# A new order of the attention steps in a hybrid encoder layer: head 2's scores behind the last key tile and the latent keys' product, head 3's scores and the transposes one product later

## The chip, the cores and the metric

The kernel runs on one core of one Trainium2 chip. The metric is the device time of one execution in microseconds (us). The names of the engines are those of the profile: PE is TensorE (PEld its weight loads), DVE is VectorE, ACT is ScalarE, POOL is GpSimd, SP issues the loads.

## The reference

Two encoder layers on one sequence of 256 tokens and 2048 features, float32. Each layer has two groups of heads that share one input projection and one output projection, and an MLP behind them. Every sub-layer is scaled and shifted by a modulation computed from the vector `c`.

```python
for l in range(DEPTH):
    mod = cond @ w_ada[l] + b_ada[l]
    sh_a, sc_a, g_a, sh_m, sc_m, g_m = [m[:, None, :] for m in jnp.split(mod, 6, axis=-1)]
    h = _rmsnorm(x) * (1.0 + sc_a) + sh_a
    proj = h @ w_in[l]                      # dq, dk, dv, cq, ckv, kr are its columns
    ...
    out_a = _diff_attention(dq, dk, dv, positions, rel_bias_table, lam, diff_subln_g[l], lambda_init)
    q = (_rmsnorm(cq, q_norm_g[l]) @ w_uq[l]).reshape(B, S, MLA_HEADS, MLA_NOPE + MLA_ROPE)
    q_nope = q[..., :MLA_NOPE]
    q_rope = _rope(q[..., MLA_NOPE:], cos[:, :, None, :], sin[:, :, None, :])
    kv = (_rmsnorm(ckv, kv_norm_g[l]) @ w_ukv[l]).reshape(B, S, MLA_HEADS, MLA_NOPE + MLA_V)
    k_nope, v_m = kv[..., :MLA_NOPE], kv[..., MLA_NOPE:]
    k_rope = _rope(kr, cos, sin)
    out_b = _mla_attention(q_nope, q_rope, k_nope, k_rope, v_m)
    x = x + g_a * (jnp.concatenate([out_a, out_b], axis=-1) @ w_o[l])
    h = _rmsnorm(x) * (1.0 + sc_m) + sh_m
    x = x + g_m * (jnp.square(jax.nn.relu(h @ w_mlp_in[l])) @ w_mlp_out[l])
return _rmsnorm(x, final_norm_g)
```

The first group is differential attention: 4 heads, each with two softmaxes over the 256 keys with a bias, of which the second, times `lam`, is taken from the first; the values are 256 wide. The second group is latent attention (MLA): 8 heads whose queries come from a normalised 512-wide latent (`w_uq`), and whose keys and values come from a normalised 256-wide latent (`w_ukv`); a part of 64 columns is rotated by position.

## The kernel before

**Layout.** Features lie on the 128 partitions and the 256 tokens along the free dimension. A float32 weight tile is loaded as 128 x 2048 (`raw`, L152, five buffers) and split in two halves of 1024 columns into a high part (`hi`, ScalarE, L140) and a remainder (`lo`, VectorE, L141), four buffers of each. A product of weights and activations is three matmuls: `hi` with the activation's high and low part and `lo` with the high part (L176 to L178, or L251 to L253 where the tokens are the output's partitions).

**adaLN sums.** The modulation is not made on TensorE. Each 128 x 2048 tile of `w_ada` is loaded (L287) into the same five `raw` buffers and multiplied and summed on VectorE (L303). Each call of `weights` first emits the sums of the tiles that are there, and by a rate (`RATE_A0`, `RATE_A2`) now and then one more load, so these sums stand among all of VectorE's other work.

**The steps of the attention.** In the function `layer` (L646):

- `col(i)` makes one 128-wide tile of the queries or keys of the differential heads; every second one ends with a copy `k` on ScalarE (L270). Tiles 0 to 5 make the keys of heads 1, 2 and 3.
- `probs(hd)`, that is `diff_probs`, makes the scores of a head (tile `psc`, L897), adds the bias and takes the row minimum on VectorE (L898), exponentials on ScalarE (L884), then on VectorE the reciprocal (L887), the factor (L904), scaling and difference (L907, L908). Its result is `a[hd]`.
- `up_k`, `up_q(0)`, `up_q(1)`, `up_r` and `up_v` are products of the latents with a loaded weight tile each: the MLA keys `kn`, the queries `qn` of heads 0 to 3 and 4 to 7, the part to be rotated `qr` (turned on TensorE with a permutation, tile `pqr`, L870, and finished on VectorE, L873 to L875), and the values `vm` (tile `pv`). The first four fill banks `pss`.
- `turn(hd)` transposes `a[hd]` on TensorE (tile `pt`, L915) and copies it to `aT` on ScalarE.
- `mla` is a list in which the three steps of the 8 MLA heads follow one another in a staggered order: `mla[0]` is head 0's scores (tile `psm`, L963 and L964, then VectorE L965, exponentials L884, and the scaling by the reciprocal on ScalarE, L968), `mla[1]` and `mla[2]` are head 1's scores and head 0's transpose, `mla[3:6]` are head 2's scores, head 1's transpose and head 0's values (tile `pom`, L980).
- `val(cg, kq)` makes the values of the differential heads from the projected input; what is left of `mla` is spread among them.

**What sets the order.** The steps are written out by hand in the order of calls. The framework's planner takes that order as a priority, simulates the engines with its own costs, and puts an instruction that is ready at its planned time ahead of one that is not; what it plans is then each engine's fixed queue. The accumulators share eight banks (`pp`), the small tiles pools of 40 (`u`) and 6 (`t`).

Of the kernel before, what the change touches and what calls it, by code (L numbers as in the profile page):

```python
# [99 lines left out]
class Trunk:  # L100
# [545 lines left out]
    def layer(self, l, acc):  # L646
# [35 lines left out]
        def col(i, out, scale):  # L682
            def f():
                if i % 2 == 0:
                    self.ps = self.bank("ps")
                self.tile_cols(self.ps[:, i % 2], io["w_t"][l, i], h)
                if i % 2:
                    out.append(self.copy(self.ps, "k", scale))
            return f

        def up_k():
            kn.extend(self.copy(ps, "kn") for ps in self.small(io["w_uk"][l], ckv, 8))

        def up_q(b):
            qn.extend(self.copy(ps, "qn", ms) for ps in self.small(io["w_uq"][l, b], cq, 4))

        def up_r():
            raw = [self.copy(ps, "qr", ms) for ps in self.small(io["w_uq"][l, 2], cq, 4)]
            qr.extend(self.rope_q(x) for x in raw)

        def up_v():
            w = self.weights(io["w_uv"][l])
            for cg in range(2):
                pss = [self.bank("pv") for _ in range(2)]
                self.tokens_by_k(pss, [[z[:, 512 * cg : 512 * cg + 512] for z in y] for y in w], ckv, True, True)
                vm.append([self.copy(ps, "vm") for ps in pss])
# [12 lines left out]
        def probs(hd):  # L719
            return lambda: a.append(self.diff_probs(l, hd, q[hd], kk[hd]))  # L720

        def turn(hd):
            return lambda: at.append(self.transposed(a[hd]))
# [15 lines left out]
        for n, (i, dst, scale) in enumerate(order):  # L739
            col(i, dst, scale)()  # L740
            if n == 0:
                cq += self.latent(cqr, self.vec[:, V_QG + 4 * l : V_QG + 4 * l + 4])
            probs(n)()
            col(i + 1, dst, scale)()
        if l:
            self.rate = RATE_A2
        up_k()
        probs(3)()
        up_q(0)
        turn(0)()  # L750
        up_r()
        turn(1)()
        mla[0]()
        up_v()
        turn(2)()
        for f in mla[1:3]:
            f()
        up_q(1)
        turn(3)()
        for f in mla[3:6]:  # L760
            f()
# [312 lines left out]
```

## Time and profile before

| | |
|---|---|
| median of 3 runs | 2240.9 us (2237.83 to 2252.52) |
| profiled execution, its own time | 2238.34 us |
| its span, first to last instruction | 2236.6 us |
| busy PE / PEld | 98% / 88% |
| busy DVE / ACT / POOL | 74% / 50% / 0% |
| chain that ended last, PE's share | 92% |
| mean granted TensorE clock | 0.997 |
| DMA | 585.53 MB, mean 262 GB/s |

A row of a timeline has the start in us, the duration, the engine, the line, the operation, the tile written and those read, the shapes and a count; in brackets stands how long the engine was idle before it, and which instruction ended that. Matmuls overlap, so a matmul's duration is longer than the distance to the next one. A row of a grouped view has the count, then busy us and the mean ns of one, then the engine's idle time before such instructions.

### The profile page before, as it was taken

To read this page: it belongs to the slowest core of one execution; us is meant where nothing else is said; L and a number is where in the kernel's file an instruction comes from. 1 tells how busy PE (TensorE), PEld (TensorE's weight loads), DVE (VectorE), ACT (ScalarE), POOL (GpSimd) and SP (SyncE) were. 2 spreads that over 40 slices of the span, in tenths; PEclk is the share of its full clock that TensorE was granted. 3 is DMA by queue.
4 is the path that set the end of the run, shared out by engine and by line. 5 is a ranking of instruction groups with operands and counts; after the bars stand their busy time and mean duration, and the time that the engine had idled before them with its cause. 6 is when DMAs were issued, how large, how long until landed. Compare 5 with 4: busy or idle time off the path is not lost.

```text
span 2236.6 us, 33121 instructions
## 1 busy us (share of the span) xinstructions
PE 2195.2 (98%) x13362; PEld 1957.4 (88%) x13362; DVE 1665.8 (74%) x2275; ACT 1117.7 (50%) x1657; POOL 1.9 (0%) x10
## 2 busy tenths in 40 slices
PE   6899999999999999999999999999999999999998
PEld 5799889998888888888899988989888888888887
DVE  7879879988878888887888776775665565565565
ACT  4445664455454355355445465544635534544553
POOL 0000000000000000000000000000000000000000
PEclk9999999999999999999999999999999999999999
DMA  9898778898888888888779666655555555555551
GB/s 387 308 380 305 271 275 315 315 349 317 322 319 308 313 313 317 310 305 315 297 265 350 248 245 224 238 210 191 200 189 188 189 188 189 188 188 188 189 188 76
DMA packets 85692, 585.53 MB, mean 262 GB/s; under 512 B 9505, under 2 KB 9889, under 8 KB 21409
## 3 DMA queue, kind: packets, MB, share of 16 engines
q1 hardware_dynamic: 85538, 583.42, 70.1%
q8 instruction: 104, 1.70, 0.3%
q14 instruction: 50, 0.41, 0.0%
HBM read 581.28 MB, written 2.10 MB: 261 GB/s over the span
## 4 chain that ended last, share of the span: by engine, by line
PE 92%; DVE 4%; ACT 1%; issue 1%; DVEq 0%; ACTq 0%
PE ps L196 42%; PE ps L197 21%; PE pk L177 4%; PE pk L176 4%; PE pk L178 4%; PE pk L240 3%; DVE ada L303 2%; PE pv L252 1%; PE pv L251 1%; PE pv L253 1%; DVE lo L141 1%; PE ps L176 1%; PE ps L177 1%; PE ps L178 1%; PE pw L533 1%
## 5 line engine op out<-in xcount | busy, mean ns | idle before, releaser
L141 DVE TENSOR_TENSOR lo<-raw,hi 128x1024 fp32r<-128x1024 f32 (+1 forms) x722 | 853.8, 1185 | 430.1 <-ACT hi L140 426.1
L140 ACT ACTIVATE hi<-raw 128x1024 fp32r<-128x1024 f32 (+1 forms) x722 | 740.2, 1028 | 824.2 <-PE ps L196 610.7
L196 PE MATMUL ps<-hid,hi 128*128 128x512 f32 x2048 | 718.0, 395 | 0.0
L196 PE MATMUL ps<-h,hi 128*128 128x512 f32 x1664 | 581.5, 394 | 0.0
L197 PE MATMUL ps<-hid,lo 128*128 128x256 f32 x2048 | 573.4, 280 | 0.0
L197 PE MATMUL ps<-h,lo 128*128 128x256 f32 x1664 | 465.7, 280 | 0.0
L196 PEld LDWEIGHTS ps<-hid,hi 128*128 128x128 f32 x2048 | 384.0, 188 | 91.6 <-DVE hid L170 1.3
L303 DVE SCALAR_TENSOR_TENSOR ada<-ada,cond 128x2048 f32<-128x2048 f32 x192 | 437.8, 2283 | 2.8 <-DMA ada<-in_w_ada 2.7
L197 PEld LDWEIGHTS ps<-hid,lo 128*128 128x128 f32 x2048 | 386.7, 189 | 0.1
L196 PEld LDWEIGHTS ps<-h,hi 128*128 128x128 f32 x1664 | 311.9, 187 | 72.6
L197 PEld LDWEIGHTS ps<-h,lo 128*128 128x128 f32 x1664 | 314.1, 189 | 0.0
L177 PE MATMUL pk<-h,hi 128*128 128x256 f32 x704 | 199.0, 283 | 0.0
L178 PE MATMUL pk<-h,lo 128*128 128x256 f32 x704 | 198.9, 283 | 0.0
L176 PE MATMUL pk<-h,hi 128*128 128x256 f32 x704 | 198.5, 284 | 0.0
L834 DVE SCALAR_TENSOR_TENSOR x<-ps,mod,x 128x256 f32<-128x256 f32 x272 | 131.2, 483 | 65.2 <-PE ps L197 60.5
L177 PEld LDWEIGHTS pk<-h,hi 128*128 128x128 f32 x704 | 135.1, 192 | 0.1
L178 PEld LDWEIGHTS pk<-h,lo 128*128 128x128 f32 x704 | 135.1, 192 | 0.0
L176 PEld LDWEIGHTS pk<-h,hi 128*128 128x128 f32 x704 | 134.6, 192 | 0.1
L240 PE MATMUL pk<-hf,w 128*128 128x256 f32 x384 | 90.0, 398 | 11.5 <-ACT hf L547 11.5
L240 PEld LDWEIGHTS pk<-hf,w 128*128 128x128 f32 x384 | 76.6, 201 | 24.0 <-ACT hf L547 12.7
L196 PE MATMUL ps<-mo,hi 128*128 128x512 f32 x192 | 69.0, 399 | 0.0
L196 PE MATMUL ps<-do,hi 128*128 128x512 f32 x192 | 68.9, 399 | 0.0
(205 smaller groups left out, 2283.8 us busy)
## 6 DMA issues: line engine op xcount, KB each, us to landing
raw<-in_w_m SPq DMA_DIRECT2D x232, 1024.0 KB, 4.9
ada<-in_w_ada SPq DMA_DIRECT2D x192, 1024.0 KB, 4.9
raw<-in_w_ob SPq DMA_DIRECT2D x24, 1024.0 KB, 5.1
raw<-in_w_m SPq DMA_DIRECT2D x32, 768.0 KB, 4.4
raw<-in_w_dv SPq DMA_DIRECT2D x16, 1024.0 KB, 4.8
raw<-in_w_a SPq DMA_DIRECT2D x20, 768.0 KB, 6.3
raw<-in_w_t SPq DMA_DIRECT2D x12, 1024.0 KB, 4.8
w<-in_w_a SPq DMA_DIRECT2D x24, 384.0 KB, 8.9
```

The lines of the kernel that those rows point to most:

```text
L140: nc.scalar.activation(hi, v, AF.Copy)
L141: ins = nc.vector.tensor_tensor(lo, v, hi.bitcast(F32), ALU.subtract)
L176: mm(ps, hi, x[0], start=first, stop=False, skip_group_check=shared)
L177: mm(ps, hi, x[1], start=False, stop=False, skip_group_check=shared)
L178: mm(ps, lo, x[0], start=False, stop=last, skip_group_check=shared)
L196: mm(ps.rearrange("p a b -> p (a b)"), hi, both, start=k == 0, stop=False)
L197: mm(ps[:, 0], lo, x, start=False, stop=k == nk - 1)
L240: self.nc.tensor.matmul(ps, v, whole[k], start=first, stop=last, skip_group_check=True)
L251: mm(ps, xh, hi, start=first and k == 0, stop=False)
L252: mm(ps, xh, lo, start=False, stop=False)
L303: ins = nc.vector.scalar_tensor_tensor(w, w, 1.0, self.cond, ALU.mult, ALU.mult, accum_out=acc[:, i : i + 1])
L834: self.nc.vector.scalar_tensor_tensor(x, ps[i][:, j], g[:, m + i : m + i + 1], x, ALU.mult, ALU.add)
```

## The change

The order of the calls in `layer`, for both layers. `probs(2)` leaves the loop, where it stood between `col(4)` and `col(5)`, and follows `up_k()`. `probs(3)` follows `up_q(0)` instead of preceding it. `up_v()` precedes `mla[0]` instead of following it, and `up_q(1)` precedes `mla[1:3]`. No call is added or left out.

```diff
             col(i, dst, scale)()
             if n == 0:
                 cq += self.latent(cqr, self.vec[:, V_QG + 4 * l : V_QG + 4 * l + 4])
-            probs(n)()
+            if n < 2:
+                probs(n)()
             col(i + 1, dst, scale)()
         if l:
             self.rate = RATE_A2
         up_k()
+        probs(2)()
+        up_q(0)
         probs(3)()
-        up_q(0)
         turn(0)()
         up_r()
         turn(1)()
+        up_v()
         mla[0]()
-        up_v()
         turn(2)()
+        up_q(1)
         for f in mla[1:3]:
             f()
-        up_q(1)
         turn(3)()
         for f in mla[3:6]:
             f()
```

## The prediction

> **What bounds the kernel now.** I read the page first: the engines' busy shares and the chain of work that ended last.
>
> ```profile
> span 2236.6 us, 33121 instructions
> PE 2195.2 (98%) x13362; PEld 1957.4 (88%) x13362; DVE 1665.8 (74%) x2275; ACT 1117.7 (50%) x1657; POOL 1.9 (0%) x10
> ...
> PE 92%; DVE 4%; ACT 1%; issue 1%; DVEq 0%; ACTq 0%
> ```
>
> TensorE sets the time: 92% of the chain is PE. A new order of the same instructions can therefore only win what PE loses by waiting, in the stretch that the edit touches: the attention of layer 0 (about 200 to 262 us) and of layer 1 (about 1288 to 1345 us). Next come sums over stretches. Columns: length, then busy time with the count for PE, PEld, DVE, ACT, POOL, then granted clock, DMA share, GB/s.
>
> ```profile
> 172.00:216.00 44.00, 44.00 (x353) 43.40 (x352) 43.54 (x82) 25.44 (x45) 0.00 (x0) 1.00 0.81 304
> 216.00:224.00 8.00, 6.16 (x43) 5.54 (x43) 5.87 (x15) 5.48 (x15) 0.00 (x0) 1.00 0.73 277
> 224.00:248.00 24.00, 22.96 (x146) 19.46 (x145) 23.03 (x40) 15.23 (x29) 0.00 (x0) 1.00 0.71 268
> 1270.00:1326.00 56.00, 55.60 (x393) 51.20 (x393) 45.40 (x93) 33.66 (x67) 0.00 (x0) 1.00 0.66 245
> ```
>
> In layer 0 PE has two weak places, 216 to 224 and 224 to 248 us, and VectorE is full on both sides of the first (43.54 of 44, 23.03 of 24). In layer 1 PE is idle for 0.40 us of 56 and VectorE has room. PE's timeline names the holes of layer 0:
>
> ```profile
> 218.63 0.28 PE L178 MATMUL pss<-lath,lo 128*128 128x256 f32 x1
> 220.45 1.13 PE L897 MATMUL psc<-k,q 128*128 128x256 f32 x4 [1.54 <-ACT k L270]
> ...
> 221.53 0.28 PE L177 MATMUL pss<-latl,hi 128*128 128x256 f32 x1
> 221.65 0.28 PE L178 MATMUL pss<-lath,lo 128*128 128x256 f32 x1
> 222.23 0.70 PE L897 MATMUL psc<-k,q 128*128 128x256 f32 x2 [0.30 <-DVE mx L898]
> ...
> 234.81 2.13 PE L870 MATMUL pqr<-qr,K 128*128 128x512 f32 x4
> ...
> 238.81 0.40 PE L253 MATMUL pv<-hi,latl 128*128 128x512 f32 x1
> 239.04 0.39 PE L251 MATMUL pv<-hi,lath 128*128 128x512 f32 x1
> 239.62 0.67 PE L964 MATMUL psm<-kr,qr 128*128 128x256 f32 x2 [0.19 <-DVE qr L875]
> ...
> 242.89 0.59 PE L964 MATMUL psm<-kr,qr 128*128 128x256 f32 x2
> ...
> 245.38 0.60 PE L963 MATMUL psm<-kn,qn 128*128 128x256 f32 x2
> 245.81 0.59 PE L964 MATMUL psm<-kr,qr 128*128 128x256 f32 x2
> 247.26 0.33 PE L915 MATMUL pt<-ident,sm 128*128 128x128 f32 x1 [0.85 <-ACT sm L968]
> ```
>
> Idle time in brackets is shorter than the loss, since a matmul's end is modelled; I count from start to start. Neighbouring rows give the pace: a 256-column product starts 0.12 us after the last one (221.53, 221.65), a pair of MLA score products takes 0.43 (245.38, 245.81), and an undisturbed `pv` product 0.23 (238.81, 239.04). So the losses are 220.45 − 218.63 − 0.12 = 1.70 us, 222.23 − 221.65 − 0.12 = 0.46, 239.62 − 239.04 − 0.23 = 0.35 and 247.26 − 245.81 − 0.43 = 1.02. In layer 1 PE's waits between 1285 and 1410 us have one entry, and its timeline has the place:
>
> ```profile
> PE pt L915 <- ACT sm L968: 0.4, 1, 0.4
> ...
> 1324.72 0.59 PE L964 MATMUL psm<-kr,qr 128*128 128x256 f32 x2
> 1325.69 0.33 PE L915 MATMUL pt<-ident,sm 128*128 128x128 f32 x1 [0.38 <-ACT sm L968]
> ```
>
> 1325.69 − 1324.72 − 0.43 = 0.54 us. The five sum to 1.70 + 0.46 + 0.35 + 1.02 + 0.54 = 4.07 us, 0.18% of the span. That is all that this edit can win.
>
> **Why PE waits at 220.45.** Head 3's scores need its keys. The last product of `col(5)` was over before the first of `up_k` at 212.15, yet ScalarE copied the keys at 219.81. The timelines of PE, VectorE and ScalarE say why:
>
> ```profile
> 212.15 0.28 PE L176 MATMUL pss<-lath,hi 128*128 128x256 f32 x1
> ...
> 215.51 2.29 DVE L303 SCALAR_TENSOR_TENSOR ada<-ada,cond 128x2048 f32<-128x2048 f32 x1
> ...
> 215.69 0.51 ACT L884 ACTIVATE s<-s,mx 128x256 f32<-128x256 f32 x1 [1.00 <-DVE mx L898]
> ...
> 218.19 0.51 ACT L884 ACTIVATE s<-s,mx 128x256 f32<-128x256 f32 x1 [1.89 <-DVE mx L898]
> ...
> 218.85 1.06 ACT L140 ACTIVATE hi<-raw 128x1024 fp32r<-128x1024 f32 x1
> 219.81 0.58 ACT L270 ACTIVATE k<-ps 128x512 f32<-128x512 f32 x1
> ```
>
> The copy stands in ScalarE's queue behind the exponentials of head 2, and the last of those waits for VectorE's row maximum, which itself stood behind an adaLN sum of 2.29 us begun at 215.51. The key copy is the victim of head 2's softmax.
>
> **The change part by part.** No instruction is added or removed and none changes its size: 4.07 us of holes is the stake, and each part only decides which holes close and which open.
>
> (1) `col(5)` and `up_k()` come before `probs(2)`. The last key tile (48 products) and the latent keys' product (48) no longer share ScalarE and VectorE with head 2's softmax. The key copy loses its cover of exponentials and can run when its bank is done, near 212; head 3's scores come after `up_k` (48 × 0.12 = 5.8 us), head 2's scores and `up_q(0)` (5.8 us), over 11 us later. That removes 1.70, and with it the 0.46, where the second half of head 3's scores waited on the first one's maximum. In layer 1 PE never waited for that copy (the one entry above is another), so nothing is won there.
>
> (2) `up_q(0)` comes before `probs(3)`. It puts 5.8 us between the scores of heads 2 and 3, where `up_k` stood before, so the two softmaxes stay as far apart as they were. Head 3's result is wanted only by `turn(3)`, behind `up_r`, `up_v` and `up_q(1)`.
>
> (3) `up_v()` comes before `mla[0]`, so 24 products at 0.23 us (5.5 us) stand whole before MLA head 0's scores, and the rotary part has that much longer. This removes the 0.35.
>
> (4) `up_q(1)` comes before `mla[1:3]`: 48 products, 5.8 us, now lie between head 0's scores and the transpose of its probabilities. The old chain there ran from 242.89 (last score product) to 247.26, 4.4 us, so it fits; that removes 1.02 in layer 0 and 0.54 in layer 1.
>
> The loads: `up_k`, `up_q`, `up_r` and `up_v` each issue one load on SP and credit the adaLN loads; the moved `probs`, `turn` and `mla` steps issue none. The order among the loads stays, so SP's queue is the same, and SP's own waits here are for VectorE to release buffers. I cost it at 0.
>
> **What opens.** VectorE's work for heads 2 and 3 now starts only after `up_k`. Its rows from 172 to 244 us, four heads:
>
> ```profile
> L898 DVE CUSTOM_DVE_ANT_0 s<-psc,bias 128x256 f32<-128x256 f32 x16 | 6.7, 416 | 1.1 <-PE psc L897 1.1
> L908 DVE SCALAR_TENSOR_TENSOR a<-s,r,s 128x256 f32<-128x256 f32 x8 | 3.5, 479 | 0.0
> L907 DVE TENSOR_SCALAR s<-s,c 128x256 f32<-128x256 f32 x8 | 2.4, 349 | 0.0
> L898 DVE DVE_READ_ACCUMULATOR2_ANT mx<- 128x1 f32 x16 | 1.3, 83 | 0.0
> L887 DVE RECIPROCAL r<-tot 128x2 f32<-128x2 f32 x8 | 1.3, 160 | 1.3 <-ACT s L884 1.3
> L904 DVE TENSOR_SCALAR c<-r,lam 128x2 f32<-128x2 f32 x4 | 0.9, 225 | 0.0
> ...
> 221.75 0.42 DVE L898 CUSTOM_DVE_ANT_0 s<-psc,bias 128x256 f32<-128x256 f32 x1
> ...
> 238.79 0.68 DVE L875 TENSOR_TENSOR qr<-qr,qrt 128x512 f32<-128x512 f32 x1
> ```
>
> One head is (6.7 + 3.5 + 2.4 + 1.3 + 1.3 + 0.9) / 4 = 4.0 us of VectorE. Before, nearly all of head 2's 4.0 us lay ahead of head 3's first reduction at 221.75 (1.3 us after its scores began at 220.45), and the half of the rotary work that MLA heads 0 to 3 need was done at 238.79 + 0.68 = 239.5. After, `up_k` ends at about 212.15 − 1.13 (the four score products that sat inside `col(5)`) + 5.8 = 216.8, and head 2's first reduction comes at 216.8 + 1.3 = 218.1. From there to the first rotary half there are the old 239.5 − 221.75 = 17.7 us and 4.0 for head 2: ready at 239.8. PE comes to MLA head 0 after head 2's scores (1.13 + 2 × 0.70 = 2.5), `up_q(0)` 5.8, head 3's 2.5, a transpose 0.4 (an estimate from the 0.33 of the row at 247.26), `up_r` 5.8, `pqr` 2.1, a transpose 0.4 and `up_v` 5.5: 216.8 + 25.0 = 241.8. So VectorE is in time by 2.0 us, a margin smaller than one adaLN sum. The new waits that I can't place are bounded by 0 below and by the return of the largest pair, 1.70 + 0.46 = 2.16 us, above; less than nothing is excluded, as the old holes are already counted as closed. Nearest is the layer 0 row itself, on a VectorE as full as then, at half its weight since the margin is positive: 1.1 us in layer 0 and 0 in layer 1.
>
> Sum: −4.07 + 1.1 = −3.0 us. The profiled execution took 2238.34 us (span 2236.6 and 1.7 around it), so it would be 2235.3; the median of the three runs, 2240.9, is 2.6 above that execution, and on its scale I forecast **2237.9 us**.
>
> **A rule that speaks against moving holes together.** In this trace a hole near 4 us costs clock too:
>
> ```profile
> 76.45 0.28 PE L376 MATMUL pl<-vec,ones 128*128 128x4 f32 x2
> 80.45 0.92 PE L240 MATMUL pk<-hf,w 128*128 128x256 f32 x3 [3.72 <-ACT hf L547]
> ...
> 80.00:84.00 4.00, 3.55 (x10) 2.89 (x11) 1.80 (x5) 3.93 (x9) 0.00 (x0) 0.67 0.97 394
> ```
>
> After it the granted clock was 0.67 for 4 us, 1.3 us lost; after the hole of 1.70 us it stayed 1.00. The Trainium skill, "TensorE: Matmul & The Clock Gate", section "Why this matters for your kernels", says to leave no idle gap over about 3 us between bursts, or the clock falls to half. The 0.67 is a mean over 4 us and agrees in direction. By that rule the sum stays as it is unless the new waits fall in one piece; then it is dearer by the clock's share, which the slower rival contains from the row above.
>
> **The rivals.** *The order is given back* (nothing happens). The program's order is only a priority for the planner: products of `up_v` already stand among MLA head 0's scores in the rows above (238.81 to 239.62), where the program has `up_v` behind them. If VectorE's queue keeps the score work late, the holes move and keep their size: −0.5, 2240.4 us. Against it: the hole at 220.45 came from the queue's order, which this edits.
>
> *VectorE becomes the bound in layer 0* (slower than before). Place: MLA head 0's scores, waiting for the rotary half. VectorE also idles while a head's exponentials and scores run: 1.3 before L887 and 1.1 before L898 in the rows above, nearly all of it in head 3's chain, 2.4 us. If both heads' chains are drawn out so after 218.1, the rotary half comes 2 × 2.4 later, at 244.6, and with an adaLN sum of 2.3 put ahead of it at 246.9: PE waits 5.1, and the clock's 1.3 from the row above makes 6.4, or 6.4 − 4.1 = +2.3 in all: 2243.2 us. It decides once the rotary half is later than 241.8 + 4.1 = 245.9. For it: VectorE's full rows. Against it: VectorE's 2.1 us idle in 216 to 224, which the move can fill.
>
> *Larger than 1%, either way*: 22.4 us would take ten holes of the size of the pair above. Nothing in the trace gives that as a gain. As a loss, only a planner whose order goes wrong through the rest of the layer could; 2265 us or more.
>
> **How the numbers follow.** Forecast 0.50, order given back 0.20, VectorE the bound 0.17, a loss over 1% 0.09, a gain over 1% 0.04. A difference of 1% is about what a measurement of this kernel can tell from no change; the first three lie inside it, 0.87. The range takes all of the first three and the scatter of the runs shown (2237.83 to 2252.52): from 2231 to 2250.
>
> **What would show it.** Right: no wait of `psc` on the key copy; that copy near 212; no wait of `pt` on `sm` at head 0 in either layer; PE's losses between 206 and 262 us down from 3.5 to near 1. Wrong: a PE wait on `qr` or on `lo` of 2 us or more near 241, a granted clock below 1.00 there, or the score products again under `up_k`.

## Result and the profile after

The changed kernel is slower: 2258.6 us, median of 8 runs (2255.95 to 2263.02), against 2239.2 us for the kernel before, timed beside it (8 runs, 2236.51 to 2252.52). The ratio is 1.0086, with a 95% interval from 1.0070 to 1.0101, which is 15.7 to 22.6 us. The forecast was 2237.9 us in a range from 2231 to 2250. The lines behind the edited loop stand two lower in the changed kernel (L897 is L899, L963 to L965 are L965 to L967, L968 is L970, L870 is L872, L915 is L917).

From its page, the span and the engines' shares:

```profile
span 2259.2 us, 33121 instructions
PE 2207.8 (98%) x13362; PEld 1963.7 (87%) x13362; DVE 1666.5 (74%) x2275; ACT 1118.1 (49%) x1657; POOL 1.9 (0%) x10
```

The instructions are the same in number, and no engine is busier by more than 13 us of the 22.6 us that this execution is longer. Where the time went is seen from marks that both kernels have: an attention begins with the first score product `psc` and is over when the output projection begins with the first `pk<-mo`. Those rows in PE's timeline, before (four rows, layer 0 and layer 1) and after:

```profile
178.57 0.46 PE L897 MATMUL psc<-k,q 128*128 128x256 f32 x1
321.86 0.47 PE L176 MATMUL pk<-mo,hi 128*128 128x256 f32 x1
1259.39 0.46 PE L897 MATMUL psc<-k,q 128*128 128x256 f32 x1
1400.22 0.47 PE L176 MATMUL pk<-mo,hi 128*128 128x256 f32 x1
```

```profile
179.37 0.46 PE L899 MATMUL psc<-k,q 128*128 128x256 f32 x1
330.69 0.47 PE L176 MATMUL pk<-mo,hi 128*128 128x256 f32 x1
1274.77 0.46 PE L899 MATMUL psc<-k,q 128*128 128x256 f32 x1
1424.39 0.47 PE L176 MATMUL pk<-mo,hi 128*128 128x256 f32 x1
```

The attention took 143.3 and 140.8 us before, and 151.3 and 149.6 after: +8.0 and +8.8, together +16.8 us, inside the interval of the ratio. The other 5.8 us of this pair lie outside the two stretches: 0.8 ahead of the first, 6.6 between them, and 1.6 the other way behind the second. The 6.6 comes back in the last section. PE's waits in the two stretches after, longest first (columns: us in total, times, longest):

```profile
PE psm L965 <- DVE sm L967: 3.5, 2, 3.3
PE pqr L872 <- ACT qr L270: 3.1, 1, 3.1
```

```profile
PE psm L965 <- DVE sm L967: 3.3, 1, 3.3
PE pqr L872 <- ACT qr L270: 2.7, 1, 2.7
```

All five old holes are gone. In their place each layer has two new ones, of 2.7 to 3.3 us: hole A, where the rotation `pqr` waits for the copies `qr`, and hole B, where the MLA scores `psm` wait for VectorE. Behind each hole the granted clock fell. Sums over the stretches (last three columns: clock, DMA share, GB/s):

```profile
234.00:242.00 8.00, 5.07 (x14) 2.84 (x15) 8.00 (x13) 3.97 (x7) 0.00 (x0) 0.79 0.95 357
260.00:264.00 4.00, 2.38 (x7) 1.92 (x8) 1.17 (x8) 2.00 (x6) 0.00 (x0) 0.58 1.00 418
264.00:268.00 4.00, 4.00 (x13) 3.26 (x12) 0.33 (x3) 1.99 (x5) 0.00 (x0) 0.57 0.10 43
1332.00:1338.00 6.00, 5.79 (x16) 3.30 (x17) 5.59 (x11) 1.24 (x3) 0.00 (x0) 0.72 0.69 251
1356.00:1360.00 4.00, 3.28 (x10) 2.78 (x11) 0.93 (x5) 1.85 (x7) 0.00 (x0) 0.57 0.88 369
```

Each row costs about 1.7 us of clock (8.00 × 0.21, 4.00 × 0.42, 4.00 × 0.43, 6.00 × 0.28, 4.00 × 0.43). Behind hole B of layer 0 there are two such rows: in the trace's record of the clock it was at 0.50 from 260.65 to 267.48 us there, and behind the other three holes for 3.41 us each. Layer 1: waits 3.3 + 2.7, clock 1.7 + 1.7, less the old 0.54, is 8.9 of 8.8 us. Layer 0: waits 3.5 + 3.1, clock 1.7 + 1.7 + 1.7, less the old 1.70 + 0.46 + 0.35 + 1.02, is 8.2 of 8.0 us. The sums come out a little high because the clock fell shortly before PE's wait was over (260.65 against 261.62), and that time is in both terms.

**Hole A** in the timelines of PE and ScalarE:

```profile
233.59 0.28 PE L178 MATMUL pss<-lath,lo 128*128 128x256 f32 x1
236.93 3.58 PE L872 MATMUL pqr<-qr,K 128*128 128x512 f32 x4 [3.06 <-ACT qr L270]
...
233.42 0.51 ACT L886 ACTIVATE s<-s,mx 128x256 f32<-128x256 f32 x1 [0.82 <-DVE mx L900]
...
233.93 1.99 ACT L140 ACTIVATE hi<-raw 128x1024 fp32r<-128x1024 f32 x2
235.82 0.57 ACT L270 ACTIVATE aT<-pt 128x512 f32<-128x512 f32 x1
236.30 1.07 ACT L270 ACTIVATE qr<-pss 128x512 f32<-128x512 f32 x2
```

`up_r` ends at 233.59. ScalarE's two copies of its result stand behind the last exponentials of head 3, two weight splits and the copy of a transpose, although the first of them needs only the first half of `up_r`.

**Hole B** in the timelines of PE and VectorE:

```profile
257.30 1.03 PE L966 MATMUL psm<-kr,qr 128*128 128x256 f32 x4
261.62 1.22 PE L965 MATMUL psm<-kn,qn 128*128 128x256 f32 x2 [3.29 <-DVE sm L967]
...
257.76 2.28 DVE L303 SCALAR_TENSOR_TENSOR ada<-ada,cond 128x2048 f32<-128x2048 f32 x1
...
259.98 0.42 DVE L967 TENSOR_SCALAR_CACHE_REDUCE sm<-psm 128x256 f32<-128x256 f32 x1
...
261.07 0.17 DVE L889 RECIPROCAL r<-tot 128x2 f32<-128x2 f32 x1 [0.67 <-ACT sm L886]
261.15 0.40 DVE L967 TENSOR_SCALAR_CACHE_REDUCE sm<-psm 128x256 f32<-128x256 f32 x1
```

The second half of a head's scores waits for the reduction of its first half. That reduction (261.15) stands in VectorE's queue behind an adaLN sum of 2.28 us, the reduction of the head before it and that head's reciprocal, which in turn waits for exponentials. PE has nothing between the two heads' scores with which to pass that time. The adaLN sum is most of the delay: without it the wait would have been near 3.3 − 2.2 = 1.1 us (an estimate from these rows, 257.76 to 259.98). No run leaves the sum out.

### The profile page after: what moved, and what is told of

Same layout as the page of the kernel before. It is cut to its first block, busy times and chain, and to the rows that moved or that the text cites. A ratio compares the mean times of both kernels' runs of the same rounds, so it can differ in the third digit from the quotient of the medians.

```text
span 2259.2 us, 33121 instructions
## 1 busy us (share of the span) xinstructions
PE 2207.8 (98%) x13362; PEld 1963.7 (87%) x13362; DVE 1666.5 (74%) x2275; ACT 1118.1 (49%) x1657; POOL 1.9 (0%) x10
## 4 chain that ended last, share of the span: by engine, by line
PE 93%; DVE 4%; ACT 1%; issue 0%; DVEq 0%; ACTq 0%
PE ps L196 42%; PE ps L197 21%; PE pk L177 4%; PE pk L176 4%; PE pk L178 4%; PE pk L240 2%; DVE ada L303 2%; PE pv L251 1%; PE pv L253 1%; PE pv L252 1%; PE ps L177 1%; PE ps L178 1%; PE ps L176 1%; DVE lo L141 1%; PE pw L533 1%; PE pom L982 1%
```

## The experiments

Each kernel was timed beside the kernel before on the same chip. "Stretches" is the time of the two attentions by the marks above, from one profiled execution of each kernel; before it is 143.3 and 140.8, as changed 151.3 and 149.6.

| kernel | median us (before beside it) | ratio, 95% interval | stretches, layers 0 and 1 |
|---|---|---|---|
| undo_q1 | 2256.95 (2243.28) | 1.0056 [1.0044, 1.0068] | 147.8, 147.5 |
| undo_p3 | 2261.82 (2243.28) | 1.0080 [1.0068, 1.0092] | 151.7, 151.5 |
| undo_both | 2260.11 (2243.28) | 1.0073 [1.0058, 1.0089] | 152.5, 151.8 |
| only_q1 | 2251.71 (2243.28) | 1.0031 [1.0020, 1.0043] | 148.2, 145.2 |
| only_p2 | 2249.61 (2243.50) | 1.0025 [1.0007, 1.0043] | 148.3, 146.2 |
| q1_cover | 2253.02 (2243.50) | 1.0034 [1.0014, 1.0053] | 146.5, 144.9 |
| r_first | 2263.25 (2243.50) | 1.0063 [1.0039, 1.0087] | 151.8, 151.8 |
| p2_col5 | 2248.12 (2243.50) | 1.0007 [0.9989, 1.0024] | 142.6, 142.5 |
| a_own | 2253.01 (2243.66) | 1.0039 [1.0027, 1.0052] | 142.9, 147.1 |
| cover_own | 2242.08 (2243.66) | 0.9987 [0.9975, 0.9999] | 140.3, 140.9 |
| before_own | 2243.65 (2243.66) | 1.0003 [0.9993, 1.0013] | 143.3, 140.6 |
| p2c5_own | 2244.11 (2243.66) | 1.0000 [0.9991, 1.0009] | 143.2, 140.4 |

The first four take the change apart. My theories on the trace alone were: hole A comes from the place of head 3's scores, whose exponentials stand ahead of the `qr` copies; hole B comes from `up_q(1)` being moved away from between `mla[1:3]` and `mla[3:6]`.

**undo_q1**: `up_q(1)` back behind `mla[1:3]`, the rest as changed.

```diff
         turn(2)()
-        up_q(1)
         for f in mla[1:3]:
             f()
+        up_q(1)
         turn(3)()
```

> The changed kernel with one part undone: up_q(1) goes back behind mla[1:3]. Measured is the stretch from the first psc product of a layer to the first product of the output projection (pk from mo): 143.3 and 140.8 us before, 151.3 and 149.6 us in the changed kernel, layers 0 and 1. Theory T (two covers were taken away): the hole of 3.5 us at psm in each layer comes from up_q(1), which was the work beside MLA head 1's softmax; it goes with the 2.8 us that the lower clock adds behind it. Stretches 145 and 143 us, time 2246 us (up to 2248 if the old 1.0 and 0.5 us at pt come back); the hole at pqr stays at about 3 us. Rival R1 (VectorE is the bound since the heads 2 and 3 start late): a hole moves but the sum stays, stretches over 149 and 147 us, 2255 us. Rival R2 (the time is lost outside the attention, by another pace in the MLP): 2258 us.

Hole A stayed as it was (first fence, layer 0). Hole B didn't close: it moved up one group, to 250.0 us, between `mla[0]` and `mla[1:3]`, where `up_v` stood before the change. The stretches are shorter all the same, since the clock didn't fall behind it (last line):

```profile
PE pqr L872 <- ACT qr L270: 3.1, 1, 3.1
PE psm L965 <- DVE sm L967: 2.8, 1, 2.8
...
250.00:254.00 4.00, 4.00 (x30) 3.85 (x31) 0.61 (x4) 3.03 (x9) 0.00 (x0) 1.00 0.91 371
```

**undo_p3**: `probs(3)` back ahead of `up_q(0)`.

```diff
         probs(2)()
-        up_q(0)
         probs(3)()
+        up_q(0)
```

> The changed kernel with one part undone: probs(3) goes back ahead of up_q(0). T: the hole of 3.2 us before pqr comes from head 3's exponentials, which stand ahead of the copies qr in ScalarE's queue; with up_q(0) between them it goes, with the 1.5 us that pqr then lost by the lower clock. Stretches 146.6 and 145 us, time 2249 us; the hole at psm stays. R1: with head 3 earlier by 5.8 us on VectorE both holes shrink, stretches near 144 and 142 us, 2243 us. R2: 2258 us.

My theory of hole A failed here. With head 3's softmax one product earlier the hole is not gone but larger, 4.2 us (3.2 in layer 1):

```profile
PE pqr L872 <- ACT qr L270: 4.2, 1, 4.2
PE psm L965 <- DVE sm L967: 3.3, 1, 3.3
```

**undo_both**: both of these, so that `probs(2)` behind `up_k` and `up_v` ahead of `mla[0]` are left.

> Both undone: only probs(2) behind up_k, and up_v ahead of mla[0], are left of the change. T: no hole above 1 us is left, and the old 1.7 and 0.5 us at psc are gone too: stretches 140 to 142 and 139.5 to 141 us, time 2236 us against 2239 before. R1: head 2's late start alone still costs, stretches over 146 and 144 us, 2248 us. R2: 2250 us or more.

Missed as well: A as in undo_p3 (4.2), B as in undo_q1 (2.9), and the time as changed. So part (1) must make A, and B belongs to whichever group has lost its product.

**only_q1**: the kernel before, with part (4) alone (`up_q(1)` ahead of `mla[1:3]`).

> The kernel before with one part of the change alone: up_q(1) ahead of mla[1:3]. T: this alone opens the hole at psm in both layers: stretches 148.6 and 146.5 us, time 2250 us; no hole at pqr. R1: heads 2 and 3 are where they were, so VectorE is not late and nothing is lost: stretches 142 to 143 and 140 us, 2238 us. R2: no forecast but a change of pace in the MLP, within 5 us of 2239 us.

Hole B comes alone, in both layers, and the old waits on the keys stay:

```profile
PE psm L963 <- DVE sm L965: 2.7, 1, 2.7
PE psc L897 <- ACT k L270: 1.4, 1, 1.4
```

**only_p2**: the kernel before, with part (1) alone.

```diff
-            probs(n)()
+            if n < 2:
+                probs(n)()
             col(i + 1, dst, scale)()
...
         up_k()
+        probs(2)()
         probs(3)()
         up_q(0)
```

> The kernel before with one part alone: col(5) and up_k() ahead of probs(2), and probs(3) right behind it; up_q(0), up_v and up_q(1) stay. Stretch from the first psc product to the first pk product of mo, as before (143.3 and 140.8 us in the kernel before). Theory U (what failed is the part that was to gain: heads 2 and 3 start late, so the copies qr of up_r stand in ScalarE's queue behind head 3's exponentials and two splits hi): the hole before pqr is there with this part alone, 3 to 4 us and 1.5 us of lower clock behind it; the old 1.7 us at psc is gone; no hole at psm. 146 to 147 and 145 us, time 2248 to 2250 us against 2240 before. Rival V (pqr waits only in company with up_v ahead of mla[0], which takes the slack): no hole, 141.5 and 140.5 us, 2238 us.

Hole A comes alone, in both layers (layer 0 has a smaller wait of `psm` on the late rotary half besides):

```profile
PE pqr L872 <- ACT qr L270: 4.1, 1, 4.1
PE psm L966 <- DVE qr L877: 1.5, 1, 1.5
```

So each hole comes with one part of the change alone. Added up, parts (1) and (4) would lengthen each stretch by nearly 10 us, where the whole change makes 8.0 and 8.8; parts (2) and (3) weren't run alone.

**q1_cover**: as changed, and a product of the differential values put where `up_q(1)` had been; it is taken from the list behind.

```diff
         for f in mla[1:3]:
             f()
+        val(0, 0)()
         turn(3)()
...
-            [val(cg, kq) for cg in range(2) for kq in range(4)],
+            [val(cg, kq) for cg in range(2) for kq in range(4)][1:],
```

> The changed kernel, with the first value product val(0, 0) (24 products of 0.23 us, 5.5 us) moved up between mla[1:3] and turn(3). Theory W (each group of MLA steps needs one product behind it; the change moved up_v and up_q(1) one place up and left none between mla[1:3] and mla[3:6]): the hole of 3.5 us at psm is gone in both layers with the 2.8 us of lower clock behind it, the hole before pqr stays: 145 and 143.5 us against 151.3 and 149.6, time 2246 us. Rival (VectorE is the bound there, not the missing cover): a hole of over 2 us stays near that place, 149 and 148 us, 2255 us.

Hole B is gone in both layers; A is all that the list of waits still has (here for layer 0):

```profile
PE pqr L873 <- ACT qr L270: 3.1, 1, 3.1
```

The adaLN sum still stands ahead of a head's reduction there, and PE doesn't wait:

```profile
258.08 2.29 DVE L303 SCALAR_TENSOR_TENSOR ada<-ada,cond 128x2048 f32<-128x2048 f32 x1
```

So another product serves there as well as `up_q(1)`, and with one in this place neither the sum nor the softmax holds PE up. The time is 2253 us and not 2246, and the stretches are 1.5 us above the expected ones.

**r_first**: as changed, with `up_r` ahead of `probs(3)`.

```diff
         up_q(0)
+        up_r()
         probs(3)()
         turn(0)()
-        up_r()
```

> The changed kernel with probs(3) behind up_r() instead of ahead of it. Theory U: the copies qr now come ahead of head 3's exponentials in ScalarE's queue, so the hole before pqr goes with its lower clock, the hole at psm stays: 146.6 and 145 us, time 2249 us. Rival X (ScalarE and VectorE simply lack time for heads 2 and 3 and the rotary part between up_k and MLA head 0): the hole moves to psm or pt of turn(3) and keeps its size, 150 us or more in both layers, 2257 us.

Hole A is gone. But MLA head 0 now waits instead (at 246.37 us in layer 0, 3.2 us): its first reduction stands behind head 3's softmax and another adaLN sum. The other of the two waits of `psm` is hole B as before (262.69, 3.3 us). These are the numbers of rival X, that VectorE and ScalarE simply lack time here; a_own and cover_own below are what speaks against it.

```profile
PE psm L965 <- DVE sm L967: 6.5, 2, 3.3
```

**p2_col5**: the kernel before, with `probs(2)` only behind `col(5)` and `up_k` behind it.

> The kernel before with only col(5) ahead of probs(2); up_k stays behind it. The key copy of head 3 then stands ahead of head 2's exponentials. Theory U: the 1.7 us and 0.5 us at psc in layer 0 go, and head 2 is late by 5.8 us only where col(5) hid it, so no hole before pqr: 141 to 142 and 140.5 us, time 2238 us. Rival (any delay of head 2 delays head 3's exponentials past the copies qr): a hole of 1.5 us or more before pqr, 144 to 146 us and 143 us, 2245 us.

Nothing in all: 1.0007. Layer 0's key hole is gone, but waits of 1.8 and 1.0 us on `psm` take its place, and layer 1 gets a small hole A of 2.3.

**a_own**: what keeps the `qr` copies behind head 3's softmax, when the program's place of it isn't the reason? The small tiles share one pool, `u`. My new theory was that the planner hands out its slots in the order of the program: a tile that is allocated behind `a` of head 3 is planned behind it, and `a` is written only at the end of head 3's softmax. `aT`, `qn` and `qr` are such tiles. So: as changed, with `a` in four slots of its own, and 36 instead of 40 in the pool.

```diff
-        self.up = pool("up", 40)
+        self.up = pool("up", 36)
...
-        a = self.u("a")
+        a = self.up.tile([P, 2, T], F32, tag="a", name=self.name("a"), bufs=4)
```

> The changed kernel with the results a of diff_probs in four slots of their own; the pool of 40 keeps 36, so the memory is the same. Theory Z (the planner hands out the slots of one pool in the order of the program: the copies aT and qr of turn(0) and up_r can't be planned before head 3's a, which is written only at the end of its softmax, so they stand behind it in ScalarE's queue; own slots free them): the hole before pqr goes in both layers with its lower clock, the hole at psm stays. Stretch from the first psc product to the first pk product of mo 146.6 and 145 us against 151.3 and 149.6, time 2249 us. Rival X (ScalarE and VectorE lack time for heads 2 and 3 between up_k and MLA head 0, whatever the slots): a hole of 2.5 us or more stays before pqr or psm, 150 us or more in layer 0, 2256 us.

The order of the program and the total of the slots are as changed; ScalarE's queue is not. In its timeline, in which the attention begins 2.3 us earlier, the first copy of `qr` comes at 228.46 instead of 236.30, and both stand ahead of the last exponentials of head 3 (232.24), which they stood behind:

```profile
228.46 0.59 ACT L270 ACTIVATE qr<-pss 128x512 f32<-128x512 f32 x1
...
231.75 0.60 ACT L270 ACTIVATE qr<-pss 128x512 f32<-128x512 f32 x1 [1.13 <-PE pss L178]
232.24 0.50 ACT L886 ACTIVATE s<-s,mx 128x256 f32<-128x256 f32 x1
```

PE's waits have nothing left on `qr` in layer 0 and 0.4 us in layer 1. Hole B stays, in layer 0 as 0.5 and 2.1 us, in layer 1 at 3.7:

```profile
PE psm L965 <- DVE sm L967: 3.7, 1, 3.7
PE pqr L872 <- ACT qr L270: 0.4, 1, 0.4
```

So the shared slots are what tied the copies to head 3's softmax. That the tie is the order in which the slots are handed out is my reading of it and not shown; nor does a run have a pool of 36 with `a` left in it.

**cover_own**: both remedies, a_own and the product of q1_cover, on top of the change.

> The changed kernel with both remedies: own slots for a, and val(0, 0) between mla[1:3] and turn(3). Z and W together: no hole above 1 us, stretches 141 to 142 and 139.5 to 140.5 us, below the 143.3 and 140.8 of the kernel before; time 2238 us against 2242. Rival X: a hole of 2.5 us or more stays in layer 0, 145 us or more, 2248 us.

```profile
178.77 0.46 PE L900 MATMUL psc<-k,q 128*128 128x256 f32 x1
319.05 0.47 PE L176 MATMUL pk<-mo,hi 128*128 128x256 f32 x1
1263.25 0.46 PE L900 MATMUL psc<-k,q 128*128 128x256 f32 x1
1404.18 0.47 PE L176 MATMUL pk<-mo,hi 128*128 128x256 f32 x1
...
PE pqr L873 <- ACT qr L270: 0.4, 1, 0.4
```

The one wait in its lists, over both layers, is 0.4 us. The attentions take 140.3 and 140.9 us: 3.0 less than before in layer 0, 0.1 more in layer 1, in all 2.9 us or 0.13%, and the ratio, 0.9987, says the same. It is the only version with an interval below 1, but the interval ends at 0.9999, which among twelve kernels is weak; the holes that are gone are the better evidence. Layer 0 is now as short as layer 1.

**before_own**: the kernel before, with `a` in slots of its own. If the theory is right, the key copy at 219.81 was late for the same reason as `qr`: the tile `k` is allocated behind `a` of head 2.

> The kernel before with own slots for a, no step moved. Z: the old wait of head 3's scores for the key copy had the same cause (the copy k is planned behind head 2's a), so the 1.7 us and 0.5 us in layer 0 go without any change of the order: 141 and 140.5 us, time 2240 us. Rival (that wait was VectorE's lateness alone): the 1.7 us stay, 143 us.

Both old waits of `psc` are gone, and the key copy comes at 214.07 us, so the reading is borne out. But a wait of 2.1 us opens at `psm`, with a lower clock behind it, and the time is the same (1.0003):

```profile
PE psm L963 <- DVE sm L965: 2.1, 1, 2.1
...
246.00:250.00 4.00, 4.00 (x20) 3.68 (x19) 3.44 (x7) 1.77 (x6) 0.00 (x0) 0.57 0.96 381
```

**p2c5_own**: p2_col5 with slots of its own for `a`.

> The kernel before with col(5) ahead of probs(2), with own slots for a. Z: the hole of 2.5 us before pqr that this order had in layer 1 goes, 140 us there; in layer 0 142 us or less; 2238 us. Rival X: the hole stays, 142.5 us in layer 1.

Layer 1's hole A is gone; in layer 0 a wait of 2.2 us at `psm` stays. The time is the same as before (1.0000).

## Why the prediction was wrong

**What bounds, and the stake.** Right: the five holes were real, all five closed, and 16.8 of the 19.4 us that the medians differ by lie in the stretches where the new order works. cover_own, with next to no wait left, gains 2.9 us of the stake of 4.07.

**Part (1), the key copy.** Right that it would come early and that the waits of `psc` would go. Wrong on the cause. The copy did stand behind late exponentials, and I blamed the adaLN sum that delayed VectorE. before_own keeps all exponentials and sums and takes that wait away by slots alone. Since I didn't ask why a ready copy is planned behind exponentials, I didn't see that the same could befall other copies allocated behind `a` of a later head. Moving head 2 behind `up_k` drew heads 2 and 3 towards the rotary product, whose copies stand in that order: hole A.

**Part (2)** was costed as neutral, and this step is the nearest to right: undo_p3 changed the stretches by 0.4 and 1.9 us only, for the better where the change has it.

**Parts (3) and (4), the failed step for hole B.** The sum took the 0.35, 1.02 and 0.54 that the moved products save at their new places, and nothing for what they leave behind. The kernel before had one product between each two groups of MLA steps: `up_v` ahead of `mla[1:3]`, `up_q(1)` ahead of `mla[3:6]`. The change moved both up by one, so the gap between `mla[1:3]` and `mla[3:6]` had only transposes. Of the moved cover I should have written what it costs where it is gone: the softmax chain of 4.4 us from the prediction's own rows (242.89 to 247.26), which no longer had 5.8 us of products over it. That was an estimate of the right size for hole B, in both layers, though by luck in part: the wait that came isn't for that chain's end but for the next head's first reduction, and an adaLN sum makes up most of it.

**What opens, the failed step for hole A.** The path of PE in the sum was right as far as the rotation: 216.8 + 2.5 + 5.8 + 2.5 + 0.4 + 5.8 = 233.8 us, and the last product of `up_r` started at 233.59. Between that and `pqr` the sum has nothing. What stood there was ScalarE's copies `qr`, at 236.30, for which PE waited 3.1 us: I counted VectorE's load and not the order in ScalarE's queue. The sum also ends at MLA head 0, ahead of the place of hole B. And I bounded the new waits by the largest old pair, 2.16 us in layer 0 and 0 in layer 1; they came to 6.6 and 6.0 us, before the clock. Layer 1 was put at 0 because VectorE has room there. Other slots and another place of one product took the holes away with the same load, so room in the mean didn't help. The sign that I had named, a wait on `qr` of 2 us or more with a lower clock, did come, by another way than the one I had in mind.

**The clock.** The warning was right and its price was left out of the sum. The price of 1.3 us was also read in a window that ended too early: from 84 to 86 us the clock was still 0.80, another 0.4 us. In the row of tile `pqr` after, and in the same row of cover_own (ns: least, median, most; then first and last start), the four products take 2.8 us from first to last start instead of 1.3:

```profile
L872 PE MATMUL pqr<-qr,K x4: 854/1061/1222, 236.9 to 239.7; 128*128 128x512 f32 x4
...
L873 PE MATMUL pqr<-qr,K x4: 590/593/684, 233.5 to 234.8; 128*128 128x512 f32 x4
```

The Trainium skill, "TensorE: Matmul & The Clock Gate", section "Why this matters for your kernels", warns of idle gaps over about 3 us. The trace of the changed kernel agrees: behind the four waits of 2.7 to 3.3 us the clock was between 0.57 and 0.79. In its two layers 8.5 us of clock (the five rows above) went with 12.6 us of waits. Below 3 us the runs differ, and there the measurement decides: the 2.1 us of before_own cost clock too (0.57), while the 2.8 and 2.9 us of undo_q1 cost none (1.00 from 250 to 254 and from 1342 to 1346 us). So the length of the wait alone doesn't decide it here, and no threshold follows from these runs.

**The rivals.** "VectorE becomes the bound" had the sign and, with an adaLN sum ahead of a reduction, part of what hole B is made of. Its place (the rotary half) and its price (+2.3 us) were wrong. The measured 2258.6 us lie between it (2243.2) and the large loss (2265 or more), so no rival had the size. That the change stayed just inside 1%, to which I had given 0.87, is luck: none of the three cases behind that number was what happened. The large loss had no mechanism: I had looked for one place that could cost 22 us, not for four places of 3 us with the clock behind them.

## What to carry to other kernels

When a step is moved up as cover, write down two prices: what it closes where it comes, and what it opens where it leaves; there the chain that it covered is to be read as if bare. When a short copy waits in an engine's queue behind work that it doesn't need, ask what ties them, the slots of a shared pool among it: tiles that are written late should not share their slots with tiles that are wanted soon. A hole of 2 to 4 us in the engine that bounds cost its length here and, behind most but not all of them, 1.7 or 3.4 us of clock.

## What the runs showed of the hardware

The MLP's products ran at one of two paces, at a granted clock of 1.00 in both. Windows of 40 us, two of before and then one of after (the count behind PE's busy time):

```profile
600.00:640.00 40.00, 40.00 (x233) 34.98 (x232) 31.89 (x40) 21.25 (x30) 0.00 (x0) 1.00 0.81 301
1000.00:1040.00 40.00, 40.00 (x229) 34.67 (x228) 32.89 (x42) 24.24 (x39) 0.00 (x0) 1.00 0.79 295
...
600.00:640.00 40.00, 40.00 (x228) 34.69 (x227) 33.59 (x41) 18.70 (x26) 0.00 (x0) 1.00 0.84 316
```

A pair of products took 346.7 or 353.3 ns from start to start, and as a rule the pace held for a whole stage between two pauses of PE, which then took 177.7 or 181.0 us, 3.3 us apart. The part between the two attentions took 937.5 us before and 944.1 after in the profiled executions, and between 935.6 and 944.3 in those of the experiments. The 6.6 us of the profiled pair are two stages that ran at the faster pace before and at the slower one after; they are less than half of the scatter of the runs of the kernel before (2236.51 to 2252.52). What chooses the pace stays open. It is the reason why the stretches were compared by their own marks, and not by the whole time.
